# Two heads of a stick-breaking pair in one 768-column tile, issued at high priority

## The chip, the cores and the metric

The kernel runs on 1 core of one Trainium2 chip. The metric is the device time of one execution in microseconds (us). Three executions of the kernel before took 410.56, 411.70 and 412.22 us; their median, 411.7 us, is the time to be compared with.

## The reference

Two layers, each a mixer sub-layer and a memory cross-attention sub-layer, on 256 tokens of 1024 columns in float32. The mixer has three groups of heads: MoBA block attention (6 heads of 64), differential attention (4 heads) and stick-breaking attention (6 heads of 64). The change touches the stick-breaking heads alone:

```python
z = jnp.einsum('bhqd,bhkd->bhqk', qi, k).astype(jnp.float32) * scale
mask = kpos[None, :] < (q0 + jnp.arange(Q_BLOCK))[:, None]
log_beta = jax.nn.log_sigmoid(z)
log_1m_beta = jnp.where(mask, log_beta - z, 0.0)
between = lax.cumsum(log_1m_beta, axis=3, reverse=True) - log_1m_beta
w = jnp.where(mask, jnp.exp(log_beta + between), 0.0)
```

The weights `w` are then multiplied with the values. Per head the kernel needs a softplus of the masked scores, its running sum along the keys, and an exponential.

## The kernel before

Every matrix product is made of three matmuls of rounded float32 parts: each operand is split into a high part (ScalarE, ACT, line 158 for weights: `whi`) and a low part (VectorE, DVE, line 159: `wlo`). Weights arrive in granules of 128x1024 numbers; `load_next` issues a granule's DMA, its `whi` and its `wlo`, five granules ahead of the one in use. The buffers `whi` and `wlo` are six deep, so that a granule's split waits until TensorE (PE) has finished with the granule six before it.

PE's order is written out by hand: the program runs under a manual schedule for PE, and jobs (generators) put small pieces of attention between the matmuls of the projections after delays given as constants (`SB_WAIT`, `SB_PACE` and so on). The orders of ACT and DVE are made by the framework's scheduler when the program is built, from the order in the source and from priorities; `self.urgent()` raises the priority of what is issued inside it. Each engine then works through its own fixed order and waits at an instruction whose inputs are not there.

Stick-breaking works on three pairs of heads per layer, in the order 1, 2, 0 of the pair index. Here they are called pair 1, 2 and 3 by that order. For each pair:

- `score_banks` (lines 547 and 548): the scores of the two heads on PE, 384 columns a head (the causal part of 256x256), in two PSUM banks.
- `stick_logs`, once per head: on DVE the mask is added (line 612, `sbz`); on ACT come Abs (613), Exp (614), Ln (615), Exp (617, into `sbr`) and Relu (618, into `sbu`); on DVE two scalar_tensor_tensor (619 and 620), two scans (622, 256 and 128 columns) and a subtraction (623, back into `sbz`). The tiles are 128x384, two buffers each.
- `p_transposed` (lines 584 and 587), some 9 us later by PE's plan: three transposes a head on PE that read `sbz`, and an ACT Exp out of PSUM into `pt`.
- `pv` (lines 595 and 597): the product with the values, and a DVE product with the gate (line 712).

These pieces lie among the matmuls of the token projections T0, T3 and T2 (lines 443 to 445), at 54 to 96 us in layer 0 and 253 to 296 us in layer 1. In the same stretch the scheduler also has to place weight splits, the rope of T0 (lines 536 to 541 on DVE), the copies out of PSUM (line 685 on ACT) and, in layer 0 alone, the norm of the memory (`rsm`, lines 329 to 338, which ends in two transposes on PE, line 385, just ahead of pair 1's six transposes).

Of the kernel before, what the change touches and what calls it, by code (L numbers as in the profile page):

```python
# [11 lines left out]
F32 = mybir.dt.float32  # L12
R = mybir.dt.float32r
I32 = mybir.dt.int32
AF = mybir.ActivationFunctionType
OP = mybir.AluOpType
# [6 lines left out]
SEG = (0, slice(0, 256)), (1, slice(256, 384))  # L23
# [56 lines left out]
class Trunk:  # L80
# [240 lines left out]
    def inv_root(self, src, mul, add, n, name):  # L321

        nc = self.nc
        W = lambda k: self.work.tile([128, n], F32, name=k + name)
        ms, y, t = W("ms"), W("rs"), W("rt")
        if mul == 1.0:
# [277 lines left out]
        self.split(self.gate[c], h, lw)  # L604
        return h, lw

    def stick_logs(self, ps):

        nc = self.nc
        W = lambda n: self.work.tile([128, 384], F32, name=n)  # L610
        z, e, y, r, u = W("sbz"), W("sbe"), W("sby"), W("sbr"), W("sbu")
        nc.vector.tensor_tensor(z, ps[:, 0:384], self.smask, OP.add)
        nc.scalar.activation(e, z, AF.Abs)  # L613
        nc.scalar.activation(e, e, AF.Exp, scale=-1.0)
        nc.scalar.activation(y, e, AF.Ln, bias=1.0)

        nc.scalar.activation(r, y, AF.Exp, scale=-1.0)
        nc.scalar.activation(u, z, AF.Relu)
        nc.vector.scalar_tensor_tensor(r, e, 1.0, r, OP.add, OP.mult)  # L619
        nc.vector.scalar_tensor_tensor(r, r, -1.0, y, OP.add, OP.add)  # L620
        for _, c in SEG:
            nc.vector.tensor_tensor_scan(y[:, c], u[:, c], r[:, c], 0.0, OP.add, OP.add)  # L622
        nc.vector.tensor_tensor(z, z, y, OP.subtract)  # L623
        return z


    def mixer(self, l):
        nc = self.nc
# [61 lines left out]
        def sb_v(h, t):  # L690
            if h < 2:
                return tok["t3"][:, t, 384 + 64 * h:448 + 64 * h]
            return sv[:, t, 64 * h - 128:64 * h - 64]

        def together(pending, last, first, then):

            pending.append((first, then))
            if last:
                outs = [f() for f, _ in pending]
                for o, (_, f) in zip(outs, pending):  # L700
                    f(o)
# [2 lines left out]

        def sb(c, last):
            qk = [x[64 * j:64 * j + 64] for j in range(2) for x in (sqk[c], sqk[3 + c])]
            z = [self.stick_logs(ps) for ps in self.score_banks(*qk)]
            yield 760, SB_WAIT
            w = [self.p_transposed(x, AF.Exp) for x in z]
            yield 660, SB_PT  # L710
            together(sbp, last, lambda: self.pv(lambda j, t: sb_v(2 * c + j, t), w),
                     lambda o: nc.vector.tensor_tensor(self.gate[5 + c], o, self.gate[5 + c], OP.mult))
            yield 720 * len(sbp) * last, 0
            if last:
                sbp.clear()


        jobs = [self.job(sb(c, i > 0), SB_START + SB_PACE * i) for i, c in enumerate((1, 2, 0))]

        def transposed(x, blocks, dst):  # L720
# [377 lines left out]
```

## Time and profile before

| | |
|---|---|
| three runs | 410.56, 411.70, 412.22 us |
| profiled execution, its own time | 411.77 us |
| its span, first to last instruction | 410.0 us |
| mean granted TensorE clock | 0.985 of full speed |
| PE busy | 392.7 us (96%) |
| DVE busy | 332.8 us (81%) |
| ACT busy | 282.4 us (69%) |

The span is 1.8 us shorter than the execution's own time; what lies around it is the start and the end of the program. The granted clock has two levels, 1.2 and 2.4 GHz; in the views 1.00 is the upper one and 0.50 the lower. A group's "idle before" is time in which the engine stood still just before an instruction of it, and the name behind the arrow is what it was waiting for. Times in a timeline are from the start of the span.

### The profile page before, as it was taken

Reading aid. Unit: us, or ns where it says so; the run is one execution under the profiler, and the core shown is the slowest. Engines: PE = TensorE matmul, PEld = TensorE weight load, DVE = VectorE, ACT = ScalarE, POOL = GpSimd, SP = SyncE. Lnnn points to the kernel's source line nnn. Section 1 sums busy time; section 2 is a strip of 40 time slices with the busy share of each in tenths; the row PEclk is TensorE's granted clock in tenths of the full one; section 3 lists DMA queues with packets and bytes.
Section 4 is the critical chain, followed back from the end, with each engine's and each line's share of the span. In section 5 each row is a group of like instructions: output and inputs, shape, how many; then the busy total and the mean of one; then the engine's idle time right before and its main releaser. Section 6 shows DMA issues by size and latency. Waiting matters only on the chain.

```text
span 410.0 us, 7670 instructions
## 1 busy us (share of the span) xinstructions
PE 392.7 (96%) x2779; PEld 353.6 (86%) x2779; DVE 332.8 (81%) x808; ACT 282.4 (69%) x593; POOL 42.5 (10%) x104
## 2 busy tenths in 40 slices
PE   8999999698999999999999999898799999999994
PEld 7999987576889989988999998675578999998983
DVE  5988869969888968889797855798789798697954
ACT  6889667667867667649476943888568677575843
POOL 3688940000000000000000000000000000000000
PEclk9999999999999999999999999999699999999998
DMA  7994783412374334621747665334225433352002
GB/s 267 351 334 163 273 272 102 152 56 83 127 254 156 102 115 144 221 89 51 257 134 269 215 217 191 102 116 146 104 104 199 161 104 116 142 171 86 2 2 103
DMA packets 19191, 64.10 MB, mean 156 GB/s; under 512 B 2384, under 2 KB 2768, under 8 KB 19152
## 3 DMA queue, kind: packets, MB, share of 16 engines
q1 hardware_dynamic: 19152, 63.61, 45.7%
q8 instruction: 22, 0.36, 0.3%
q14 instruction: 17, 0.14, 0.1%
HBM read 62.55 MB, written 1.05 MB: 155 GB/s over the span
## 4 chain that ended last, share of the span: by engine, by line
PE 71%; DVE 15%; ACT 8%; issue 4%; DMA 1%; SPq 0%; DVEq 0%; ACTq 0%
PE bank L416 38%; PE bank L443 4%; PE bank L444 4%; PE bank L445 4%; DVE wlo L159 3%; DVE sby L622 3%; PE bank L973 3%; PE bank L584 2%; PE bank L595 2%; ACT whi L158 2%; DVE sbr L620 1%; PE bank L908 1%; DVE sbr L619 1%; ACT sbe L613 1%; DVE sbz L623 1%
## 5 line engine op out<-in xcount | busy, mean ns | idle before, releaser
L159 DVE TENSOR_TENSOR wlo<-wraw,whi 128x1024 fp32r<-128x1024 f32 (+2 forms) x118 | 136.9, 1169 | 33.5 <-ACT whi L158 33.0
L158 ACT ACTIVATE whi<-wraw 128x1024 fp32r<-128x1024 f32 (+2 forms) x118 | 117.9, 1010 | 39.5 <-PE bank L416 19.5
L416 PE MATMUL bank<-xh,whi 128*128 128x256 f32 x416 | 119.3, 288 | 0.1
L416 PE MATMUL bank<-xh,wlo 128*128 128x256 f32 x416 | 117.5, 284 | 0.2 <-DVE wlo L159 0.2
L416 PE MATMUL bank<-xl,whi 128*128 128x256 f32 x416 | 117.3, 283 | 0.0
L416 PEld LDWEIGHTS bank<-xh,whi 128*128 128x128 f32 x416 | 79.6, 192 | 1.6 <-issue 0.7
L416 PEld LDWEIGHTS bank<-xh,wlo 128*128 128x128 f32 x416 | 79.6, 192 | 0.5 <-DVE wlo L159 0.4
L416 PEld LDWEIGHTS bank<-xl,whi 128*128 128x128 f32 x416 | 79.6, 192 | 0.0
L443 PE MATMUL bank<-whi,xh 128*128 128x512 f32 x128 | 54.2, 423 | 0.0
L444 PE MATMUL bank<-wlo,xh 128*128 128x512 f32 x128 | 51.3, 401 | 0.0
L445 PE MATMUL bank<-whi,xl 128*128 128x512 f32 x128 | 51.0, 399 | 0.0
L574 ACT ACTIVATE prob<-prob,mx 128x256 f32<-128x256 f32 (+1 forms) x56 | 24.8, 446 | 12.9 <-DVE mx L571 12.9
L443 PEld LDWEIGHTS bank<-whi,xh 128*128 128x128 f32 x128 | 24.8, 194 | 7.0 <-issue 2.2
L445 PEld LDWEIGHTS bank<-whi,xl 128*128 128x128 f32 x128 | 24.8, 193 | 5.6
L444 PEld LDWEIGHTS bank<-wlo,xh 128*128 128x128 f32 x128 | 24.9, 194 | 4.2
L587 ACT ACTIVATE pt<-bank 128x384 f32<-128x384 f32 x32 | 15.0, 480 | 12.6 <-PE bank L584 11.3
L302 ACT ACTIVATE xh<-h 128x256 fp32r<-128x256 f32 x32 | 14.5, 497 | 6.8 <-DVE h L298 6.3
L416 PE MATMUL bank<-mh,whi 128*128 128x256 f32 x64 | 18.8, 294 | 0.0
L416 PE MATMUL bank<-ml,whi 128*128 128x256 f32 x64 | 18.1, 283 | 0.0
L416 PE MATMUL bank<-mh,wlo 128*128 128x256 f32 x64 | 18.1, 283 | 0.0
L569 DVE CUSTOM_DVE_ANT_0 prob<-bank,cmask 128x256 f32<-128x256 f32 (+1 forms) x56 | 17.9, 351 | 0.0
L313 ACT ACTIVATE sq<-h 128x256 f32<-128x256 f32 x28 | 11.4, 410 | 6.4 <-DVE sqacc L314 5.9
(272 smaller groups left out, 781.1 us busy)
## 6 DMA issues: line engine op xcount, KB each, us to landing
wraw<-in_w_dram SPq DMA_DIRECT2D x107, 512.0 KB, 3.7
wraw<-in_w_dram SPq DMA_DIRECT2D x10, 256.0 KB, 4.4
wraw<-in_memT_dram SPq DMA_DIRECT2D x4, 512.0 KB, 4.9
h<-in_xT_dram SPq DMA_DIRECT2D x3, 256.0 KB, 5.2
out_dram<-wraw SPq DMA_DIRECT2D x2, 288.0 KB, 2.2
wraw<-in_gfin_dram SPq DMA_DIRECT2D x1, 512.0 KB, 5.4
out_dram<-wraw SPq DMA_DIRECT2D x2, 224.0 KB, 2.2
h<-in_xT_dram SPq DMA_DIRECT2D x1, 280.0 KB, 3.1
```

Source lines behind the costliest of these rows:

```text
L158: nc.scalar.activation(hi[:, c], raw[:, c], AF.Copy)
L159: nc.vector.tensor_tensor(lo[:, c], raw[:, c], hi[:, c].bitcast(F32), OP.subtract)
L302: nc.scalar.activation(h, src[k], AF.Copy, scale=g)
L416: nc.tensor.matmul(outs[m], st[:, kk, c], x[k], start=k + p == 0 and m % 2 == 0, stop=k == n - 1 and p == 2, skip_group_check=True)
L443: nc.tensor.matmul(outs[t], xh[k][:, c], whi[:, kk, :], start=first, stop=False)
L444: nc.tensor.matmul(outs[t], xh[k][:, c], wlo[:, kk, :], start=False, stop=False)
L445: nc.tensor.matmul(outs[t], xl[k][:, c], whi[:, kk, :], start=False, stop=last)
L569: nc.vector.tensor_tensor_reduce(s[:, c], ps[:, c], self.cmask[:, c], 1.0, -3.0e38, OP.add, OP.max, accum_out=m[:, t:t + 1])
L574: nc.scalar.activation(s[:, c], s[:, c], AF.Exp, bias=m[:, t:t + 1], scale=scale, accum_out=sm[:, t:t + 1])
L587: nc.scalar.activation(pt[:, 0:384], ps[:, 0:384], func)
L622: nc.vector.tensor_tensor_scan(y[:, c], u[:, c], r[:, c], 0.0, OP.add, OP.add)
L973: nc.tensor.matmul(out[:, 0:w], x[:, r], w_, start=m == 0 and not seeded, stop=m == 11, skip_group_check=True)
```

## The change

`stick_logs` is called once per pair instead of once per head. Its five tiles are 128x768 with one buffer each instead of 128x384 with two; columns 0 to 383 are the first head's and 384 to 767 the second's. The mask is still added per head and the scans are still four a pair; Abs, Exp, Ln, Exp, Relu, the two scalar_tensor_tensor and the subtraction are one instruction a pair. All of it is inside `self.urgent()`. The subtraction writes `sbr` instead of `sbz`, and the transposes read `sbr`.

```diff
-    def stick_logs(self, ps):
-
-        nc = self.nc
-        W = lambda n: self.work.tile([128, 384], F32, name=n)
+    def stick_logs(self, banks):
+
+
+        nc = self.nc
+        W = lambda n: self.work.tile([128, 768], F32, name=n, bufs=1)
         z, e, y, r, u = W("sbz"), W("sbe"), W("sby"), W("sbr"), W("sbu")
-        nc.vector.tensor_tensor(z, ps[:, 0:384], self.smask, OP.add)
-        nc.scalar.activation(e, z, AF.Abs)
...
+        with self.urgent():
+            for j, ps in enumerate(banks):
+                nc.vector.tensor_tensor(z[:, 384 * j:384 * j + 384], ps[:, 0:384], self.smask, OP.add)
+            nc.scalar.activation(e, z, AF.Abs)
+            nc.scalar.activation(e, e, AF.Exp, scale=-1.0)
+            nc.scalar.activation(y, e, AF.Ln, bias=1.0)
+
+            nc.scalar.activation(r, y, AF.Exp, scale=-1.0)
+            nc.scalar.activation(u, z, AF.Relu)
+            nc.vector.scalar_tensor_tensor(r, e, 1.0, r, OP.add, OP.mult)
+            nc.vector.scalar_tensor_tensor(r, r, -1.0, y, OP.add, OP.add)
+            for j in range(2):
+                for _, c in SEG:
+                    c = slice(384 * j + c.start, 384 * j + c.stop)
+                    nc.vector.tensor_tensor_scan(y[:, c], u[:, c], r[:, c], 0.0, OP.add, OP.add)
+            nc.vector.tensor_tensor(r, z, y, OP.subtract)
+        return r[:, 0:384], r[:, 384:768]
...
-            z = [self.stick_logs(ps) for ps in self.score_banks(*qk)]
+            z = self.stick_logs(self.score_banks(*qk))
```

PE's order stays as it was, row for row; those of ACT and DVE move. The lines of `stick_logs` have new numbers in the changed file: 615 mask, 616 Abs, 617 Exp, 618 Ln, 620 Exp into `sbr`, 621 Relu, 622 and 623 scalar_tensor_tensor, 627 scans, 628 subtraction. Lines 158 and 159 are the weight splits in both.

ACT in layer 0, pair 1, before: the ten activations of the two heads (`sbe`, `sby`, `sbr`, `sbu`) stand together, and the first weight split comes behind them.

```order
L613 ACTIVATE sbe<-sbz 128x384
L618 ACTIVATE sbu<-sbz 128x384
L614 ACTIVATE sbe<-sbe 128x384
L613 ACTIVATE sbe<-sbz 128x384
L615 ACTIVATE sby<-sbe 128x384
L614 ACTIVATE sbe<-sbe 128x384
L617 ACTIVATE sbr<-sby 128x384
L615 ACTIVATE sby<-sbe 128x384
L618 ACTIVATE sbu<-sbz 128x384
L617 ACTIVATE sbr<-sby 128x384
L330 ACTIVATE rsm<-msm 128x2
L158 ACTIVATE whi<-wraw 128x1024
```

The same place of ACT in the changed kernel, up to the copies of T0 into `tq`:

```order
L616 ACTIVATE sbe<-sbz 128x768
L621 ACTIVATE sbu<-sbz 128x768
L617 ACTIVATE sbe<-sbe 128x768
L158 ACTIVATE whi<-wraw 128x1024
L618 ACTIVATE sby<-sbe 128x768
L330 ACTIVATE rsm<-msm 128x2
L158 ACTIVATE whi<-wraw 128x1024
L620 ACTIVATE sbr<-sby 128x768
L331 ACTIVATE rsm<-rsm 128x2
L690 ACTIVATE tq<-bank,rsx 128x512 x2
```

Two weight splits have moved from behind the activations to between them: one ahead of Ln, one ahead of the second Exp.

DVE in layer 0, pair 1, before, from the first scalar_tensor_tensor on; the rest of the second head follows below it, with one `wlo` ahead of its subtraction:

```order
L619 SCALAR_TENSOR_TENSOR sbr<-sbe,sbr 128x384
L329 TENSOR_SCALAR msm<-ssm 128x2
L620 SCALAR_TENSOR_TENSOR sbr<-sbr,sby 128x384
L619 SCALAR_TENSOR_TENSOR sbr<-sbe,sbr 128x384
L622 SCALAR_TENSOR_TENSOR sby<-sbu,sbr 128x256
L622 SCALAR_TENSOR_TENSOR sby<-sbu,sbr 128x128
L620 SCALAR_TENSOR_TENSOR sbr<-sbr,sby 128x384
L335 TENSOR_TENSOR rtm<-rsm 128x2
L623 TENSOR_TENSOR sbz<-sbz,sby 128x384
L336 TENSOR_TENSOR rtm<-rtm,msm 128x2
L622 SCALAR_TENSOR_TENSOR sby<-sbu,sbr 128x256
L337 TENSOR_SCALAR rtm<-rtm 128x2
```

The same place of DVE in the changed kernel (`rp` is the rope of T0, which reads `tq`); below it stand two more scans, then `rtm`, `rp`, the subtraction, and only then `rsm`:

```order
L329 TENSOR_SCALAR msm<-ssm 128x2
L159 TENSOR_TENSOR wlo<-wraw,whi 128x1024 x2
L622 SCALAR_TENSOR_TENSOR sbr<-sbe,sbr 128x768
L335 TENSOR_TENSOR rtm<-rsm 128x2
L536 TENSOR_TENSOR rp<-tq,cosr 128x128
L623 SCALAR_TENSOR_TENSOR sbr<-sbr,sby 128x768
L336 TENSOR_TENSOR rtm<-rtm,msm 128x2
L537 TENSOR_TENSOR rp<-tq,sinr 128x128
L627 SCALAR_TENSOR_TENSOR sby<-sbu,sbr 128x256
L627 SCALAR_TENSOR_TENSOR sby<-sbu,sbr 128x128
```

Two `wlo` now stand ahead of the first scalar_tensor_tensor, two rope products among the chain, and the norm's last row has moved behind the subtraction.

DVE in layer 1, pair 2, in the changed kernel:

```order
L159 TENSOR_TENSOR wlo<-wraw,whi 128x1024 x3
L622 SCALAR_TENSOR_TENSOR sbr<-sbe,sbr 128x768
L623 SCALAR_TENSOR_TENSOR sbr<-sbr,sby 128x768
L159 TENSOR_TENSOR wlo<-wraw,whi 128x1024
L627 SCALAR_TENSOR_TENSOR sby<-sbu,sbr 128x256
L627 SCALAR_TENSOR_TENSOR sby<-sbu,sbr 128x128
L627 SCALAR_TENSOR_TENSOR sby<-sbu,sbr 128x256
L627 SCALAR_TENSOR_TENSOR sby<-sbu,sbr 128x128
L628 TENSOR_TENSOR sbr<-sbz,sby 128x768
```

Three `wlo` stand ahead of the chain's first row and a fourth ahead of its scans (before, between the pair's masks and its last subtraction, there were three: one ahead of the first head's rows and two among the second head's). In layer 0 the fourth one stands between the scans and the subtraction.

## Rows read from the trace of the kernel before

**Rows 1.** The page, busy us of each engine (share of the span) and instructions.

```profile
PE 392.7 (96%) x2779; PEld 353.6 (86%) x2779; DVE 332.8 (81%) x808; ACT 282.4 (69%) x593; POOL 42.5 (10%) x104
```

**Rows 2.** What PE waited for: us in total, times, longest us.

```profile
PE bank L584 <- DVE sbz L623: 8.4, 4, 3.5
```

**Rows 3.** Timeline of PE, layer 0: start us, us, instruction, [idle before <- releaser].

```profile
66.81 0.38 PE L385 MATMUL bank<-ident,rsm 128*128 128x128 f32 x2
67.03 0.97 PE L584 MATMUL bank<-ident,sbz 128*128 128x128 f32 x6
...
75.81 0.52 PE L584 MATMUL bank<-ident,sbz 128*128 128x128 f32 x3
79.82 0.69 PE L584 MATMUL bank<-ident,sbz 128*128 128x128 f32 x3 [3.50 <-DVE sbz L623]
...
90.97 0.82 PE L584 MATMUL bank<-ident,sbz 128*128 128x128 f32 x6
...
94.28 0.81 PE L595 MATMUL bank<-pt,t 128*64 128x256 f32 x3 [1.12 <-ACT pt L587]
```

**Rows 4.** Timeline of PE, layer 1.

```profile
264.94 0.49 PE L584 MATMUL bank<-ident,sbz 128*128 128x128 f32 x3
266.66 0.52 PE L584 MATMUL bank<-ident,sbz 128*128 128x128 f32 x3 [1.23 <-DVE sbz L623]
...
276.68 0.49 PE L584 MATMUL bank<-ident,sbz 128*128 128x128 f32 x3
278.04 0.52 PE L584 MATMUL bank<-ident,sbz 128*128 128x128 f32 x3 [0.87 <-DVE sbz L623]
...
285.82 0.52 PE L584 MATMUL bank<-ident,sbz 128*128 128x128 f32 x3
289.14 0.88 PE L584 MATMUL bank<-ident,sbz 128*128 128x128 f32 x3 [2.80 <-DVE sbz L623]
```

**Rows 5.** Stretches: length, busy us (count) of PE, PEld, DVE, ACT, POOL; PEclk; DMA.

```profile
80.00:82.00 2.00, 2.00 (x9) 1.82 (x9) 1.84 (x3) 1.45 (x4) 0.00 (x0) 0.52 0.76 248
...
84.00:86.00 2.00, 2.00 (x20) 1.47 (x17) 1.13 (x3) 1.23 (x3) 0.00 (x0) 1.00 0.09 35
...
293.00:295.00 2.00, 2.00 (x10) 1.29 (x7) 1.19 (x8) 1.15 (x6) 0.00 (x0) 0.50 0.35 127
295.00:298.00 3.00, 3.00 (x14) 2.50 (x13) 1.81 (x7) 1.06 (x1) 0.00 (x0) 0.98 0.22 90
```

**Rows 6.** Timeline of DVE, pair 1 of layer 0: the masks, the last subtraction.

```profile
57.29 1.01 DVE L612 TENSOR_TENSOR sbz<-bank,smask 128x384 f32<-128x384 f32 x2
66.78 0.55 DVE L623 TENSOR_TENSOR sbz<-sbz,sby 128x384 f32<-128x384 f32 x1
```

**Rows 7.** Timeline of ACT, weight splits in layer 0.

```profile
73.66 2.00 ACT L158 ACTIVATE whi<-wraw 128x1024 fp32r<-128x1024 f32 x2
75.97 1.06 ACT L158 ACTIVATE whi<-wraw 128x1024 fp32r<-128x1024 f32 x1 [0.31 <-PE bank L445]
```

**Rows 8.** Groups by line and shape: busy us, mean ns of one, idle before.

```profile
L159 DVE TENSOR_TENSOR wlo<-wraw,whi 128x1024 fp32r<-128x1024 f32 x107 | 129.9, 1222 | 29.9 <-ACT whi L158 29.5
L158 ACT ACTIVATE whi<-wraw 128x1024 fp32r<-128x1024 f32 x107 | 111.7, 1054 | 37.6 <-PE bank L416 19.5 <-PE bank L445 6.5 <-DMA wraw<-in_w_dram 6.0
...
L622 DVE TENSOR_TENSOR_SCAN sby<-sbu,sbr 128x256 f32<-128x256 f32 x12 | 8.3, 688 | 0.2
L620 DVE SCALAR_TENSOR_TENSOR sbr<-sbr,sby 128x384 f32<-128x384 f32 x12 | 6.7, 554 | 0.2
...
L159 DVE TENSOR_TENSOR wlo<-wraw,whi 128x512 fp32r<-128x512 f32 x9 | 6.1, 691 | 0.7 <-ACT whi L158 0.6
L615 ACT ACTIVATE sby<-sbe 128x384 f32<-128x384 f32 x12 | 6.1, 509 | 0.0
...
L158 ACT ACTIVATE whi<-wraw 128x512 fp32r<-128x512 f32 x9 | 5.5, 620 | 0.3 <-DMA wraw<-in_w_dram 0.3
L622 DVE TENSOR_TENSOR_SCAN sby<-sbu,sbr 128x128 f32<-128x128 f32 x12 | 4.8, 401 | 0.0
```

More of the change, by code (lines that the diff above doesn't have):

```diff
@@ L605, in split_merged @@
         return h, lw
-    def stick_logs(self, ps):
+    def stick_logs(self, banks):
         nc = self.nc
-        W = lambda n: self.work.tile([128, 384], F32, name=n)
+        W = lambda n: self.work.tile([128, 768], F32, name=n, bufs=1)
         z, e, y, r, u = W("sbz"), W("sbe"), W("sby"), W("sbr"), W("sbu")
-        nc.vector.tensor_tensor(z, ps[:, 0:384], self.smask, OP.add)
-        nc.scalar.activation(e, z, AF.Abs)
[L614 to L624, printed above, removed]
+        with self.urgent():
[14 more added lines that the diff above has]
+        return r[:, 0:384], r[:, 384:768]
     def mixer(self, l):
```

## The prediction

> **What bounds the kernel now.** I read the page's busy times first: PE is busy 96% of the span, DVE 81%, ACT 69% [rows 1]. So time goes where PE stands still, and the second view is PE's waits: the largest by far is its wait for the stick-breaking logs, 8.4 us in four waits [rows 2]. The third view, PE's timeline, shows where. Pair 1 of layer 0 has no such wait: its six transposes start at 67.03 [rows 3], and the second head's log ends at 66.78 + 0.55 = 67.33, just as they reach it [rows 6]. Pair 2 waits 3.50 us between its heads, pair 3 not at all [rows 3]. In layer 1 the waits are 1.23, 0.87 and 2.80 us [rows 4]. The reader should see that in each of these waits the first three transposes had gone before it: the first head was ready earlier.
>
> The fourth view is the granted clock. Behind the 3.50 us of idling PE runs at the lower level (0.52 of full speed, 1.2 GHz) and is back at 1.00 by 84; behind the 2.80 us it is at 0.50 until about 295 [rows 5]. Behind 1.23 and 0.87 us I see no fall. So a wait of about 3 us costs a half-speed stretch of 3.3 to 5.9 us as well, that is 1.7 to 2.9 us of lost time, or a little less where other waits lie in it.
>
> **The change, durations first.** An instruction of 768 columns is not in the trace. Below and above it stand 512 and 1024 columns: ACT 620 and 1054 ns, DVE 691 and 1222 ns [rows 8]. With 384 columns (509 and 554 ns) the three lie on a line of 0.85 ns a column on ACT and 1.04 on DVE, so I take 0.84 us on ACT and 0.95 on DVE. The next instruction starts some 0.1 us before the end when it doesn't need the result (two masks take 1.01 us, two splits 2.00) [rows 6, 7], so a step is 0.73 us on ACT and 0.87 on DVE. A weight split takes a step of 0.95 on ACT and 1.13 on DVE. The four scans (0.69 and 0.40 us each head, less overlap) take 1.95 us.
>
> The saving in work is small: ten activations of 0.41 us become five of 0.73 (0.45 us a pair), four scalar_tensor_tensor and two subtractions of 0.46 become three steps of 0.87 (0.15 us). ACT and DVE are not the bound, so by itself this is worth nothing. What counts is when the last subtraction lands, because PE waits there in its fixed order.
>
> **Pair 1, layer 0.** The masks end at 57.29 + 1.01 = 58.30, as before. On ACT: Abs 58.35, Relu 59.08, Exp 59.81, then by the new order a split 60.54, Ln 61.49, 0.1 for the norm's row, a split 62.31, the second Exp 63.26 to 64.1. On DVE two low parts of those splits stand ahead of the chain; the second can start only when its high part ends, 63.40 to 64.62. Then scalar_tensor_tensor 64.55 to 65.50, one rope row, the next 65.72 to 66.68, two small rows, scans to 68.8, two small rows, subtraction 69.03 to 69.98. The norm's last row now follows it, so the two norm transposes that stood at 66.81 come at 70.1 and the six of this pair at 70.3 instead of 67.03 [rows 3]: PE is 3.3 us late by a wait that was not there. By the rows above a wait of this size brings the clock down. At half speed PE needs 1.0 us for the six transposes, and while that lasts (I take 3.3 us) it loses 1.3 to 1.7 us more.
>
> **Pair 2, layer 0.** PE reaches its transposes at 75.81 + 3.3 + 1.3 = 80.4. Its masks are behind pair 1's subtraction, its Abs behind pair 1's two Exp out of PSUM: Abs 71.8, Exp 73.3, split 74.2, Ln 75.2. The next split needs the buffer of a granule that PE, itself late, leaves at about 76.9 (such a wait for PE is in the trace already, 0.31 us [rows 7]): split 77.0, second Exp 78.0 to 78.8. Then its low part to 79.3, two scalar_tensor_tensor to 81.2, scans to 83.1, a low part to 84.2, subtraction to 85.1. Before, the second half of the transposes started at 79.82 [rows 3]; now all six start at 85.15, and six take 0.5 us longer than three at that clock. PE is 5.8 us late; a fall of the clock follows as it did before.
>
> **Pair 3, layer 0.** Its DVE rows stand behind the gate products, which follow PE, in both kernels. From there it took two heads of about 2.7 us each; now it is 2.9 for two scalar_tensor_tensor and the subtraction, 1.95 and a low part of 1.13, some 0.6 us longer, and the second head had no slack at 90.97. Late by 6.4; of the 1.12 us that PE waited for `pt` at 94.28 about 0.3 goes. **Layer 0: +6.2 us**, rounded over the steps.
>
> **Layer 1**, walked the same way. Pair 1: the chain from the masks to the subtraction is that of layer 0 without the norm's row; it ends at 268.05. PE stands from 264.94 to 268.1 in place of the 1.23 us before 266.66 [rows 4]: six transposes behind it, 1.9 us late, and the clock falls where it didn't, 1.7 us more. PE reaches pair 2 at 276.68 + 3.6 = 280.2. There Abs is at 269.4, the two splits inside wait for PE's buffers (271.9 and 274.8), the second Exp ends at 276.6, the third and fourth low parts cost 0.5 and 1.1 us, and the subtraction ends at 282.95: a wait of 2.8 us, with another fall of the clock, against the end of a 0.87 us wait at 278.04. PE goes on 4.95 + 0.5 us late from the transposes and some 1.5 us more from the clock: +6.9. Pair 3 follows PE through its gates and the scores of the differential heads, one of whose rows now stands inside its chain; it ends at 296.2 against 289.14, and six transposes instead of three add 0.4. From here the clock is low in both kernels. **Layer 1: +7.5 us.**
>
> Sum: 6.2 + 7.5 = 13.7 us on the profiled execution's own 411.77 us (its span is 410.0), which is 425.5. That execution stands 0.07 us from the median of the three runs, so nothing is corrected; I say 425. Past 96 and past 296 us PE's order and nearly all of the others' are as before, and PE has no waits worth naming, so I carry the lateness to the end unchanged. The one buffer a tile costs nothing: the next pair's first writer is behind the last reader in the order anyway. DMAs are not moved.
>
> **A rule weighed.** In the trace the first head's three transposes passed before each of the four waits [rows 3, 4], while one tile holds all six back; that is the 0.4 to 0.5 us a pair in my sums. The Trainium skill says in "Perfetto Trace Analysis", section Optimizing Scalar/DVE Operations, that where these engines aren't saturated but cause bubbles on others, splitting instructions may let work finish sooner; the change does the reverse. The trace agrees with it on both conditions. The same section says that larger operations improve throughput if the engine is saturated; by that the 0.6 us of work saved a pair would be a gain of up to 3.6 us in all, but at 81% and 69% busy nothing here shows that it would reach the end.
>
> **Rivals.** (a) Faster: precedence does its work and no split lengthens the chain. From the first mask the bare chain is 1.0 for the masks, 4 x 0.84 plus the Relu between (0.6) on ACT, 3 x 0.98 and 1.95 on DVE, 10.0 us: pair 1 ends at 67.3 and 265.7 and costs nothing, pair 2 at 77.5 and 275.9, so that 3.5 us shrinks to 1.7 and 0.87 to nothing; pair 3 of layer 1 gains some 3 us. With two falls of the clock gone (4 us) that is some 10 us, 402. It decides from a chain below about 11 us. Against it: the splits do stand inside, and on ACT they start the moment the row ahead is issued. (b) Slower by less: the new waits of 3.3, 3.1 and 2.8 us leave the clock up. Then the buffers come free sooner and some 4 us go: 421. For it: the falls seen hang on single waits of 2.8 and 3.5 us. (c) Slower by more: each low stretch lasts 5.9 us, as in layer 1, 1.3 us more at four places: 430. (d) Only pair 1 loses in each layer (3.3 + 1.9 us) and pairs 2 and 3, whose scores come early, give the rest back: 417. Against it is that pair 2's masks wait for pair 1's subtraction.
>
> **How the numbers follow.** Forecast 0.58, (b) 0.18, (c) 0.10, (d) 0.06, (a) 0.05, no difference 0.03. About 0.5% (2 us) is what a measurement of this kernel can tell from no change. Cases of 417 and more are slower: 0.92; same 0.03; faster 0.05. The range takes in (b), (d) and (c): 416 to 431. The bounds of 768 columns (0.62 to 1.05 and 0.69 to 1.22 us) would move each chain by 1.6 us either way, but three points on one line leave little of that, some 2 us a layer at most.
>
> **What would show it.** In the changed profile: PE's wait for `sbr` of line 628 at six transposes in one piece, with idle times near 3.3 and 4.7 us in layer 0 and 3.1, 2.8 and 3.5 in layer 1, 15 us or more in all instead of 8.4; ACT's split rows between Exp and Ln; 0.84 and 0.95 us for 768 columns; a low clock at about 71 and 269, where it was high. I am wrong if pair 1's subtraction ends before 68 us, if PE's total of that wait falls below 8 us, or if the stretch from 96 us on gives the time back.

## The result, and the profile after

The changed kernel takes 425.12 us (median of six executions, 421.57 to 425.80) against 410.50 of the kernel before (six, 407.95 to 412.22): a ratio of 1.0352, 95% interval 1.0315 to 1.0389. It is 14.6 us slower; 425 was forecast.

The profiled execution of the changed kernel is its shortest, 421.57 us with a span of 419.6 and a mean granted clock of 0.983. The other five take 424.63 to 425.80 us at 0.971 each. So the trace shows the waits, and the clock of one execution in six.

The page after, busy us of each engine, the row that answers to [rows 1]:

```profile
PE 393.1 (94%) x2779; PEld 354.4 (84%) x2779; DVE 331.4 (79%) x790; ACT 279.5 (67%) x563; POOL 40.7 (10%) x104
```

PE runs the same 2779 matmuls, DVE and ACT do a little less than before, and the span is 9.6 us longer. What PE waited for (us in total, times, longest) answers to [rows 2]:

```profile
PE bank L584 <- DVE sbr L628: 11.0, 4, 4.5
PE bank L584 <- DVE mx L571: 4.3, 1, 4.3
PE bank L385 <- DVE rsm L338: 3.1, 1, 3.1
```

The three rows are one kind of wait: 18.4 us at the transposes, where 8.4 were before. The 3.1 is at the norm's two transposes, just ahead of pair 1's six, and the norm's row now stands behind the chain on DVE. The 4.3 is put down to `mx`, a row right behind the last subtraction on DVE. On PE's timeline after, layer 0 [rows 3] and then layer 1 [rows 4]:

```profile
70.05 0.41 PE L385 MATMUL bank<-ident,rsm 128*128 128x128 f32 x2 [3.10 <-DVE rsm L338]
70.29 1.02 PE L584 MATMUL bank<-ident,sbr 128*128 128x128 f32 x6
85.10 1.51 PE L584 MATMUL bank<-ident,sbr 128*128 128x128 f32 x6 [4.48 <-DVE sbr L628]
...
96.99 0.87 PE L584 MATMUL bank<-ident,sbr 128*128 128x128 f32 x6 [0.57 <-DVE sbr L628]
...
273.69 0.85 PE L584 MATMUL bank<-ident,sbr 128*128 128x128 f32 x6 [2.97 <-DVE sbr L628]
...
287.15 0.85 PE L584 MATMUL bank<-ident,sbr 128*128 128x128 f32 x6 [2.95 <-DVE sbr L628]
...
299.67 1.51 PE L584 MATMUL bank<-ident,sbr 128*128 128x128 f32 x6 [4.35 <-DVE mx L571]
```

Each wait now stands ahead of six transposes in one piece. Where they come from stands on ACT's timeline, pair 1 of layer 0 after (start us, us, instruction):

```profile
58.32 0.85 ACT L616 ACTIVATE sbe<-sbz 128x768 f32<-128x768 f32 x1 [2.23 <-DVE sbz L615]
...
59.80 0.83 ACT L617 ACTIVATE sbe<-sbe 128x768 f32<-128x768 f32 x1
60.54 1.04 ACT L158 ACTIVATE whi<-wraw 128x1024 fp32r<-128x1024 f32 x1
61.48 0.83 ACT L618 ACTIVATE sby<-sbe 128x768 f32<-128x768 f32 x1
...
62.31 1.04 ACT L158 ACTIVATE whi<-wraw 128x1024 fp32r<-128x1024 f32 x1
63.26 0.83 ACT L620 ACTIVATE sbr<-sby 128x768 f32<-128x768 f32 x1
```

Two splits stand inside the chain, one on each side of Ln. On DVE's timeline, the same pair, the chain goes on:

```profile
63.39 1.23 DVE L159 TENSOR_TENSOR wlo<-wraw,whi 128x1024 fp32r<-128x1024 f32 x1 [0.55 <-ACT whi L158]
64.53 0.95 DVE L622 SCALAR_TENSOR_TENSOR sbr<-sbe,sbr 128x768 f32<-128x768 f32 x1
...
66.82 1.90 DVE L627 TENSOR_TENSOR_SCAN sby<-sbu,sbr 128x256 f32<-128x256 f32 x4
...
68.88 0.95 DVE L628 TENSOR_TENSOR sbr<-sbz,sby 128x768 f32<-128x768 f32 x1
69.75 0.15 DVE L338 TENSOR_TENSOR rsm<-rsm,rtm 128x2 f32<-128x2 f32 x1
```

The subtraction ends at 69.83; before, the second head's ended at 67.33 [rows 6]. The clock after, over stretches behind the waits (columns as in [rows 5]):

```profile
72.00:74.00 2.00, 2.00 (x6) 1.61 (x5) 0.91 (x1) 2.00 (x4) 0.00 (x0) 0.50 0.13 14
...
85.00:87.00 2.00, 1.90 (x9) 1.93 (x10) 1.01 (x2) 0.98 (x2) 0.00 (x0) 0.50 0.76 262
...
274.00:276.00 2.00, 2.00 (x13) 1.70 (x12) 2.00 (x5) 1.76 (x4) 0.00 (x0) 1.00 0.03 8
287.00:289.00 2.00, 1.85 (x14) 1.74 (x15) 1.03 (x3) 1.29 (x3) 0.00 (x0) 1.00 0.00 0
299.00:301.00 2.00, 1.33 (x7) 1.36 (x8) 2.00 (x12) 1.02 (x3) 0.00 (x0) 0.61 0.10 39
```

It went down to the lower level behind the waits of 3.10 and 4.48 us, fell behind that of 4.35 as well, and stayed up behind 2.97 and 2.95.

### The profile page after: what moved, and what is told of

It reads as the page before. It is cut to its first block, busy times and chain, and to the rows that moved or that the text cites. A ratio compares the mean times of both kernels' runs of the same rounds, so it can differ in the third digit from the quotient of the medians.

```text
span 419.6 us, 7622 instructions
## 1 busy us (share of the span) xinstructions
PE 393.1 (94%) x2779; PEld 354.4 (84%) x2779; DVE 331.4 (79%) x790; ACT 279.5 (67%) x563; POOL 40.7 (10%) x104
## 4 chain that ended last, share of the span: by engine, by line
PE 71%; DVE 15%; ACT 9%; issue 3%; ACTq 0%; DVEq 0%
PE bank L416 37%; PE bank L443 4%; PE bank L444 4%; PE bank L445 4%; DVE wlo L159 4%; ACT whi L158 3%; PE bank L978 3%; PE bank L584 3%; DVE sby L627 2%; PE bank L595 2%; PE bank L913 1%; DVE sbr L628 1%; DVE sbr L622 1%; DVE sbr L623 1%; ACT sby L618 1%
## 5 line engine op out<-in xcount | busy, mean ns | idle before, releaser
L574 ACT ACTIVATE prob<-prob,mx 128x256 f32<-128x256 f32 (+1 forms) x56 | 24.8, 445 | 15.3 <-DVE mx L571 15.3
L584 PE MATMUL bank<-ident,sbr 128*128 128x128 f32 x36 | 6.6, 333 | 15.3 <-DVE sbr L628 11.0
L584 PEld LDWEIGHTS bank<-ident,sbr 128*128 128x128 f32 x36 | 4.9, 168 | 17.4 <-issue 16.4
```

What stands on the lines that cost most here:

```text
L574: nc.scalar.activation(s[:, c], s[:, c], AF.Exp, bias=m[:, t:t + 1], scale=scale, accum_out=sm[:, t:t + 1])
L584: nc.tensor.transpose(ps[:, b * 128:b * 128 + 128], p[:, b * 128:b * 128 + 128], self.ident)
```

## The experiments

Theory 1 is the prediction's: one wide chain is a row of dependent instructions, the scheduler puts weight splits into its gaps, the subtraction lands later, PE waits at a fixed place and its clock falls. The rivals: the high priority does the harm; the width does it by itself; the fixed place of the transposes matters more than the chain; the clock adds nothing.

**e1_splits_behind.** The changed kernel with the later splits held behind each pair's chain by order-only dependencies, which fix the order on an engine and carry no data (`whi` behind the second Exp on ACT, `wlo` behind the subtraction on DVE):

```diff
-                    nc.scalar.activation(hi[:, c], raw[:, c], AF.Copy)
-                    nc.vector.tensor_tensor(lo[:, c], raw[:, c], hi[:, c].bitcast(F32), OP.subtract)
+                    self.behind(nc.scalar.activation(hi[:, c], raw[:, c], AF.Copy), 0)
+                    self.behind(nc.vector.tensor_tensor(lo[:, c], raw[:, c], hi[:, c].bitcast(F32), OP.subtract), 1)
```

> The changed kernel with one thing more: every weight split that is issued after a pair's logs is ordered behind that pair's second Exp on ACT and behind its subtraction on VectorE. Tile width and priority stay. Theory 1 (the splits between the rows lengthen the chain): pair 1's subtraction ends at about 67.5 us in layer 0 instead of 69.8, its wait on TensorE falls from 3.1 to under 2 us, all the waits for the logs from some 18 us to under 10, and the time to 403 to 412 us. Theory 2 (the wide tile itself costs it, since both heads come late together): the waits stay above 14 us and the time above 420 us.

406.99 us, ratio 0.9913 [0.9876, 0.9951]: under the kernel before, 18 us under the changed one. Lines have moved by a few numbers (591 is 584, 622 is 615, 625 is 618, 627 is 620, 635 is 628, 392 and 345 are 385 and 338). PE's waits:

```profile
PE bank L591 <- DVE sbr L635: 5.1, 4, 2.3
...
PE bank L392 <- DVE rsm L345: 1.0, 1, 1.0
```

ACT, pair 1 of layer 0, from Ln on:

```profile
59.35 0.85 ACT L625 ACTIVATE sby<-sbe 128x768 f32<-128x768 f32 x1
60.23 0.84 ACT L627 ACTIVATE sbr<-sby 128x768 f32<-128x768 f32 x1
60.98 1.05 ACT L159 ACTIVATE whi<-wraw 128x1024 fp32r<-128x1024 f32 x1
```

And DVE, the masks and the subtraction of that pair:

```profile
55.95 1.02 DVE L622 TENSOR_TENSOR sbz<-bank,smask 128x384 f32<-128x384 f32 x2 [0.62 <-PE bank L554]
...
65.03 0.96 DVE L635 TENSOR_TENSOR sbr<-sbz,sby 128x768 f32<-128x768 f32 x1
```

From the first mask to the subtraction's end the chain takes 65.99 - 55.95 = 10.04 us, the 10.0 of rival (a); in the changed kernel it is 69.83 - 57.27 = 12.56. The chain also starts 1.3 us sooner, because the low part that stood just ahead of the masks is held back too: of the 3.84 us by which the subtraction comes earlier, 2.5 are the chain's. The waits at the transposes fall from 18.4 to 6.1 us. The tile of 768 columns is the same, so width by itself costs little; the splits in and ahead of the chain cost the time.

**e2_heads_priority.** The kernel before, with its two calls of 384 columns and `stick_logs` inside the priority:

```diff
+        with self.urgent():
+            nc.vector.tensor_tensor(z, ps[:, 0:384], self.smask, OP.add)
...
+            nc.vector.tensor_tensor(z, z, y, OP.subtract)
```

> The kernel before with the priority alone: per-head tiles of 384 columns with two buffers, the rows of the logs at high priority. Theory 1 (one wide chain leaves gaps that the scheduler fills with splits; two heads fill each other's): no split stands inside the chain, pair 1's second subtraction ends near 66.5 us, the waits for the logs fall from 8.4 to 2 to 5 us with no fall of the clock in the stretch, 400 to 404 us. Theory 3 (priority itself is what delays other work): 415 us or more. No change at all: 408 to 412.

407.76 us, ratio 0.993 [0.9894, 0.9966]: faster than before, but 3.8 us above the range expected. Its lines from the mask on have numbers one higher than in the kernel before. DVE, pair 1 of layer 0:

```profile
61.41 1.03 DVE L620 SCALAR_TENSOR_TENSOR sbr<-sbe,sbr 128x384 f32<-128x384 f32 x2 [0.24 <-ACT sbr L618]
62.36 1.02 DVE L621 SCALAR_TENSOR_TENSOR sbr<-sbr,sby 128x384 f32<-128x384 f32 x2
...
65.11 1.00 DVE L624 TENSOR_TENSOR sbz<-sbz,sby 128x384 f32<-128x384 f32 x2
...
66.10 1.22 DVE L159 TENSOR_TENSOR wlo<-wraw,whi 128x1024 fp32r<-128x1024 f32 x1
```

No split stands in the chain, here or in the other five pairs: each head's row fills the gap of the other's. The second head alone doesn't do this, nor the priority alone: in the kernel before, without the priority, low parts stand among the second head's rows, and in the changed kernel, with it, splits stand in the wide chain. But the norm's rows now come behind two low parts (its transposes wait 1.95 us, and the clock falls behind that wait, which was not expected), and in layer 1 the masks of pair 3 (277.43 us) come behind three (from 274.03). Its waits on PE:

```profile
PE bank L584 <- DVE sbz L624: 3.7, 1, 3.7
PE bank L385 <- DVE rsm L338: 2.0, 1, 2.0
```

So the precedence works on two interleaved chains and pushes something else late; that second part was missing in the expectation.

**e3_wide_no_priority.** The changed kernel without the priority:

```diff
-        with self.urgent():
+        with nullcontext():
```

> The changed kernel without the priority: 768-column tiles with one buffer alone. Theory 1 (the width puts the splits into the chain): as slow as the changed kernel, 421 to 428 us, with pair 1's wait at 3 us or more. Theory 3 (priority is what costs): back at 408 to 413 us.

423.25 us, ratio 1.0305 [1.0269, 1.0341], a time as expected; its interval overlaps that of the changed kernel. Pair 1's wait was expected at 3 us or more and is 2.82, now at the six transposes themselves, since the norm's rows come earlier. The order of this kernel on ACT has the same two splits inside the chain (at 61.13 and 63.00 us), at nearly the same times as in the changed kernel. PE's largest wait:

```profile
PE bank L584 <- DVE sbr L628: 13.6, 5, 4.6
```

Priority is not what slows the kernel, nor does it keep the splits out. The trace of the changed kernel fits the reason that theory 1 gives: its first split starts at 60.54 us, while Exp, on which the chain's next row depends, runs until 60.63.

**e4_heads_priority_norm.** e2 with two edits for what came late in it: the norm's rows get a still higher priority, and the subtraction writes `sbr`, so that the next masks needn't wait for the transposes.

```diff
-        with self.urgent():
+        with self.tc.high_priority(offset=1200):
             ss = self.work.tile([128, 2], F32, name="ss" + name)
...
-        nc.vector.tensor_tensor(z, z, y, OP.subtract)
-        return z
+            nc.vector.tensor_tensor(r, z, y, OP.subtract)
+        return r
```

> Per-head tiles at high priority as in e2, and two things that e2's trace showed late: the memory norm's rows get a still higher priority, and the subtraction writes sbr, so that the next pair's masks needn't wait for the transposes that read sbz. Theory 1 (only where a chain's last row lands counts): the norm's transposes and all pairs' transposes wait under 2 us in all, and the time is 399 to 403 us. If the two late things were not the cause of what e2 missed, it stays at 406 to 409 us.

406.38 us, ratio 0.9896 [0.9864, 0.9928]: above the range expected, and in the 406 to 409 us that stood for the other case, in which the two late things are not what e2 missed. By time it is not to be told from e2. The waits for the logs are gone (0.3 us is left), and others have come:

```profile
PE bank L595 <- ACT pt L587: 3.7, 3, 2.0
PE bank L726 <- DVE tq L541: 2.1, 2, 1.3
...
PE bank L584 <- DVE sbr L624: 0.3, 1, 0.3
```

So the two late things did cause those waits, but taking the waits away gained little time: PE reaches the product with `pt` sooner and waits there instead, since its place too is fixed; and T0's rope is pushed back. e9 tests the first of these two; the second was not tested.

**e5_filled_waits.** The changed kernel with twelve matmuls on zeros ahead of the six transposes, into a bank that these overwrite, for pair 2 of layer 0 and all pairs of layer 1. They add work on PE, so only the clock can gain by them; ACT and DVE keep their orders but for a few rows behind pair 2 of layer 0.

```diff
+        for i in range(fill):
+            nc.tensor.matmul(ps[:, 0:256], self.warm[:, 0:128], self.warm, start=True, stop=True)
```

> The changed kernel with 12 matmuls of 256 columns on zeros, into the bank that the transposes then overwrite, ahead of the six transposes of pair 2 in layer 0 and of all three pairs in layer 1, where TensorE otherwise stands idle for 2.9 to 4.5 us. They take 1.3 us inside the wait, so the logs come no earlier. If the falls of the clock behind the waits are what separates the executions at 425 us from the profiled one at 421.6 us, the granted clock stays up behind these four waits and the median falls to 418 to 422 us. If the falls don't hang on the idling, it stays at 424 us or more.

419.44 us (418.88 to 420.68), ratio 1.023 [1.018, 1.0281]: 5.7 us under the changed kernel. Stretches behind the filled places, the last one behind pair 3 of layer 1:

```profile
84.00:88.00 4.00, 4.00 (x32) 3.01 (x32) 1.35 (x3) 3.49 (x7) 0.00 (x0) 1.00 0.36 129
273.00:277.00 4.00, 4.00 (x20) 3.28 (x19) 1.98 (x2) 4.00 (x6) 0.00 (x0) 1.00 0.37 131
286.00:290.00 4.00, 4.00 (x27) 2.79 (x26) 0.85 (x2) 4.00 (x8) 0.00 (x0) 1.00 0.00 0
298.00:303.00 5.00, 5.00 (x22) 3.42 (x21) 3.57 (x20) 3.67 (x16) 0.00 (x0) 0.70 0.27 90
```

At three of the four places the clock stays up, and the time falls although PE has more to do. So the clock is a term of its own: the twelve matmuls at each place, their own work deducted, give 5.7 us back. The changed kernel's one trace can't divide this by places, since in it the clock was up behind two of the four already, and in e5's it is up behind pair 1 of layer 0 too, where nothing was filled. The kernel is still some 9 us slower than the one before, with 13.8 us of waits left at the transposes.

**e6_wide_norm_splits_behind.** e1 with the norm's rows at the higher priority (the first line of e4's edit).

> e1 (wide tile, priority, splits ordered behind the chain) with the memory norm's rows at a higher priority. Theory 1: the 1.0 us wait of the norm's transposes goes, pair 1 costs nothing, 404 to 407 us against 407.0 in e1. The wide chain keeps its waits at pairs 2 and 3 (0.6 to 2.3 us in e1), so it stays above e4.

407.66 us, ratio 0.9922 [0.9892, 0.9953], just above the range and not to be told from e1. The norm's wait of 1.0 us is gone, and the waits for the logs grew from 5.1 to 6.4 us: PE reaches pair 2 sooner and waits there 2.17 us, where it was 0.96 in e1.

**e7_later_transposes.** The changed kernel, with the transposes placed later in PE's plan:

```diff
-SB_WAIT, SB_PACE, SB_PT = 9000, 9000, 1300
+SB_WAIT, SB_PACE, SB_PT = 12500, 9000, 1300
```

> The changed kernel with SB_WAIT 12500 in place of 9000: TensorE's own order has the six transposes of a pair about 3.5 us of matmuls later, the splits stay inside the chains. Theory 1 (the loss is the wait at a fixed place of TensorE's order): the waits for the logs fall from some 15 us to under 6 us and the time to 405 to 414 us. If the late chain delays what follows it anyway (values, gates, the differential heads), 418 us or more.

415.41 us (413.75 to 418.17), ratio 1.0149 [1.0074, 1.0223]: between the two expectations. Waits of 4.7 us for the logs and 1.4 at `mx` are left of 15.3, but the norm's 3.1 us stay, since its transposes have their own place in the plan, and the clock falls behind them (PE's timeline, then a stretch of the clock):

```profile
70.29 0.40 PE L385 MATMUL bank<-ident,rsm 128*128 128x128 f32 x2 [3.09 <-DVE rsm L338]
```

```profile
73.00:75.00 2.00, 2.00 (x7) 1.44 (x6) 0.14 (x1) 0.62 (x1) 0.00 (x0) 0.51 0.39 117
```

So with the splits still inside the chains, moving the fixed place takes 9.7 us off the changed kernel. That is not a share of the 14.6 us: the kernel before waited 8.4 us at the same place, and what the same move would take off it was not run.

**e8_splits_behind_later and e9_heads_priority_pt_later.** Two of the four versions that came out under both kernels, each with the piece at which PE still waited moved later: e1 with `SB_WAIT` 11500 for 9000, and e4 with `SB_PT` 3300 for 1300.

> The kernel with the splits held behind the chains, with the transposes 2500 of PE's plan units later (11500 for 9000). Its PE still waited 5.1 us for the logs in four waits of 1 to 2.3 us. Theory 1 (what is left of those waits is lost time because PE's order is fixed, and other matmuls stand ready to fill it): the waits for the logs fall below 1.5 us and the time is 402 to 405.5 us. Rival (the last head's chain ends the stretch wherever the transposes stand, or the wait passes on to the exponentials and the differential heads behind): 406 us or more, with the waits at pt or mx grown by 2 us or more.

> Before's heads of 384 columns with the stick-breaking chain and the memory's norm ahead of the splits, and the product with the values placed 2000 plan units later behind the transposes (3300 for 1300). There PE waited 3.7 us for pt in three waits, and 2.1 for the rope of T0. Theory 1: the waits for pt fall below 1 us and the time is 402 to 405.5 us. Rival: the wait passes on to the rope or to the differential heads, 406 us or more.

404.44 us (404.20 to 404.59), ratio 0.9871 [0.9815, 0.9928], and 403.48 us (403.36 to 405.70), ratio 0.9861 [0.9807, 0.9914], both within theory 1's range. In e8 the waits for the logs are 1.2 us. In e9 PE's waits for `pt`, 3.7 us in e4, are gone, and one for the differential heads has come, as its rival said, though smaller than what went:

```profile
PE bank L560 <- ACT dT L728: 2.3, 1, 2.3
PE bank L726 <- DVE tq L541: 2.1, 2, 1.3
```

e9 has the lowest median, 1.4% under the kernel before, with the same work in heads of 384 columns; e8, with the wide tile, is not to be told from it. Part of this gain is the clock: the four executions of each have mean granted clocks of 0.991 to 0.999 (e9) and 0.997 to 0.999 (e8), the seven of the kernel before beside them 0.983 to 0.996. The gains of e1, e2, e4, e6, e8 and e9 are clear of the noise by their intervals, and all are under 2%.

## Why the prediction was right, step by step

- *The number.* That 425 met 425.12 is in part luck. It was 13.7 us on an execution of 411.77; six executions of the kernel before have a median of 410.50, so the step measured is 14.6. The base was 1.3 us too high and the step 0.9 too small.
- *Durations.* 768 columns were put at 0.84 and 0.95 us. The groups of the changed kernel (mean ns of one) give 834 to 844 ns on ACT and 954 to 956 on DVE; the line through 384, 512 and 1024 columns held.
- *Pair 1, layer 0.* The subtraction was forecast to end at 69.98 and ends at 69.83; the wait 3.3 us, measured 3.10; the fall of the clock is there (0.50 from 72).
- *Pair 2, layer 0.* Subtraction forecast 85.1, measured 84.95; wait 4.7 forecast, 4.48 measured. The split that waits for PE's buffer stands at 76.86, where 77.0 was said.
- *Layer 0.* Forecast +6.2. On PE's timeline layer 1's first scores start 5.6 us later, first before and then after:

```profile
253.33 0.37 PE L547 MATMUL bank<-sqk,sqk 64*128 64x128 f32 x1
```

```profile
258.94 0.37 PE L547 MATMUL bank<-sqk,sqk 64*128 64x128 f32 x1
```

- *Layer 1.* Forecast +7.5. The profiled execution shows 419.6 - 258.94 = 160.7 us from those scores to the end, against 410.0 - 253.33 = 156.7: +4.0. The first two waits are as forecast (2.97 and 2.95 for 3.1 and 2.8), the third is larger (4.35 for 3.5). What is missing is the clock behind the first two, 1.7 + 1.5 us in the forecast: in this execution it stays at 1.00. That is rival (b) for two of the three waits that it names, and its 421 is near the 421.57 of this execution, though here layer 0 came out 0.6 us under the forecast as well.
- *The whole.* The other five executions have a lower mean clock, 0.971 for 0.983, and take 3.1 to 4.2 us longer. That the clock fell in them behind those two waits fits the 3.2 us of the forecast, but not the mean clocks: 2 x (0.983 - 0.971) x 420 us is some 10 us more at the lower level, where each of the three falls in this trace lasts some 3.4 us (a mean of 0.72 over 70 to 76 us, for one), so it is nearer to three more falls than to two. No trace of one of the five is at hand: where the clock falls in them, and with it the last 3 to 4 us of the sum, stays open. e5 shows only that keeping it up is worth 5.7 us in the usual execution.
- *Rival (a)* failed as the prediction said, by the splits in the chain. e1 takes them out and gets the bare chain of 10.0 us (the terms listed for it add up to 9.85). It comes to 407 and not 402, with 6.1 us of waits at the transposes left, where the rival had 1.7 at pair 2 and hardly any elsewhere; with 2.2 left (e8) it is 404.4.
- *Rival (d)* failed: pairs 2 and 3 gave nothing back in layer 0.
- *The cause, sharpened.* The prediction charged 0.4 to 0.5 us a pair to six transposes held back by one tile. That was a small part: e1 keeps the tile and is no slower than e2, which has two (406.99 and 407.76 us, intervals that overlap). Two heads with e1's dependencies were not run; the nearest pair, e4 and e6, is not to be told apart either. The rule of the Trainium skill weighed there ("Perfetto Trace Analysis", section Optimizing Scalar/DVE Operations, that breaking up instructions may let work finish sooner) held in sign. But the runs show its way here to be another than the size of the pieces: with the same precedence two half-width chains keep the splits out (e2), and one wide chain lets them in.

What the prediction didn't see: the same precedence on two heads makes the kernel faster, and with the norm ahead, the subtraction into `sbr` and one constant changed (e9) the gain is 6 to 7 us (1.4% by the ratio, 7.0 us by the medians).

## What to carry to other kernels

When dependent instructions are merged into wider ones, count the gaps that a second, independent chain used to fill, and look in the engines' order at what fills them now; a priority doesn't keep foreign work out of a gap in which the chain has nothing ready. Where an engine waits at a place fixed by hand, its gain from a faster chain can pass on to the next such place, as it did in e4, so move the places along with the chain. Price a wait of PE with the clock behind it, and read the clock of more than the one execution that has a trace.

## What the runs showed of the hardware

The length of a single wait did not settle whether TensorE's clock falls. It stayed at 1.00 behind waits of 2.97 and 2.95 us in the changed kernel, and in e5 behind the 3.10 us of pair 1 that wasn't filled, the same wait as in the changed kernel, where it fell. At pair 1 of layer 1 in e3 it fell behind 2.97 us (0.50 from 274 to 276 us), where the changed kernel waited as long and it stayed up. In e2 it fell behind 1.95 us at the norm's transposes:

```profile
68.00:70.00 2.00, 0.99 (x9) 1.02 (x10) 2.00 (x9) 0.22 (x1) 0.00 (x0) 1.00 0.76 254
70.00:72.00 2.00, 2.00 (x7) 1.50 (x6) 2.00 (x5) 2.00 (x6) 0.00 (x0) 0.51 0.85 262
```

And here is e5 behind its 3.10 us:

```profile
70.00:72.00 2.00, 1.64 (x12) 1.55 (x13) 2.00 (x9) 0.88 (x3) 0.00 (x0) 1.00 0.03 8
72.00:74.00 2.00, 2.00 (x10) 1.64 (x9) 1.21 (x2) 2.00 (x3) 0.00 (x0) 1.00 0.00 0
```

One and the same program, the changed kernel, ran at mean clocks of 0.983 and 0.971, 3.1 to 4.2 us apart. The prediction's estimate, a fall behind every wait of about 3 us, came near the usual time, but in the one execution with a trace it held at three of five places.
